# Six 1024x1024 projections as seven half-size block products, z and gates ahead of the mixers

## The chip, the cores and the metric

The kernel runs on one core of one Trainium2 chip. Its time is device microseconds (us), the median of three runs: 1177.52 us before the change (1177.08 to 1180.14). The engines of the core are TensorE (PE; PEld is its weight load), VectorE (DVE), ScalarE (ACT), GpSimd (POOL) and SyncE (SP), which issues DMAs. Each runs its own instructions in the order in which they stand, and waits at an instruction until what it reads is there.

## The reference

One layer over 512 tokens of width 1024, in fp32 (cut to what matters):

```python
h = rms_norm(x, mixer_norm)
(q, k, v, g_out, a_lr, z, xbc, dt_raw, gate_a, gate_b) = split_cols(h @ w_in, IN_SPLITS)
o_a = gla_mixer(q, k, v, g_out, a_lr, ...)          # 4 heads, chunks of 64
o_b = ssd_mixer(z, xbc, dt_raw, ...)                # 4 groups, chunks of 128
#   in it: dt = softplus(dt_raw + bias), cumulative sums of dt * a
#   y = (y_diag + y_off + X * d_skip) * silu(z); a norm per group
merged = sigmoid(gate_a) * (o_a @ w_branch_a) + sigmoid(gate_b) * (o_b @ w_branch_b)
x = x + merged @ w_out
# a conv-gated MLP, a gated per-layer embedding and a last norm follow
```

z is 2048 columns wide, each gate 1024; w_branch_a and w_out are 1024x1024, w_branch_b 2048x1024.

## The kernel before

Every matmul of a projection is done in three passes: weights and activations are split into a high and a low fp32r part (`wsplit`, L164 on ScalarE and L165 on VectorE for the weights), and high x high, high x low and low x high are summed in PSUM. `proj_a` has weights as the stationary operand and gives features by tokens, `proj_b` has tokens as the stationary operand and gives tokens by features. A projection of 1024x1024 is 192 matmuls of 512 columns. Weights come from DRAM into buffers named raw, from SyncE's queue.

`strassen` does a 1024x1024 block in seven products of half-size blocks (24 matmuls each) instead of eight: it needs sums of weight quarters (L325 on GpSimd, or an adding DMA) and sums of activations by token halves (`combine`, L293 to L302). In this kernel only the down projection of the MLP uses it.

The order: norm and transposes of x (h1); the first four x tiles of group 0 and the dt columns (psdt); on VectorE a chain of some twenty operations from psdt to the decays (L726 to L757), a transpose of its result (psq, L761), its copy qt (L762) and a small product (pscd, L764); then per group the core `ssd_core` (per chunk: yo, yd and st on TensorE; the state S is handed from chunk to chunk), `ssd_z` (the z columns of that group, `proj_b`), `ssd_branch` of the group before (ob), and `ssd_gate` (product with silu(z), a norm on GpSimd, transposes ot into ob). Then GLA with two pairs of heads (att, kst, o, u, oaT; the norms ors on GpSimd), the merge gates (`gate_pair`, whose second gate is multiplied with accb on GpSimd, L977), `branch_pair`, and w_out.

The order on each engine is made by a scheduler from the order in the code and from priorities: `ahead(n)` puts what stands in it forward by n steps, and where an instruction waits, ready work of lower priority is put before it. The buffers of a pool limit what can be put forward: four PSUM banks (mm_ps) for projections, four (sm_ps) for all else and for the block products, four weight splits.

## Time and profile before

| what | value |
|---|---|
| median of three runs | 1177.52 us |
| the profiled execution's own time | 1180.49 us |
| its span | 1178.5 us |
| TensorE busy, share | 1157.1 us, 98% |
| VectorE busy, share | 677.4 us, 57% |
| ScalarE busy, share | 520.5 us, 44% |
| GpSimd busy, share | 171.1 us, 15% |
| DMA, mean | 100 GB/s |

The profile is of one execution; its span is 2.0 us shorter than that execution's time. A busy share is an average over stages. A matmul's own duration in a group of the profile overlaps with its neighbours', so the pace of matmuls is read from how many a window holds. What an engine waited for stands in brackets in the timeline, and the chain of waits goes from the last instruction back to what released it.

### The profile page before, as it was taken

Reading aid. Unit: us, or ns where it says so; the run is one execution under the profiler, and the core shown is the slowest. Engines: PE = TensorE matmul, PEld = TensorE weight load, DVE = VectorE, ACT = ScalarE, POOL = GpSimd, SP = SyncE. Lnnn points to the kernel's source line nnn. Section 1 sums busy time; section 2 is a strip of 40 time slices with the busy share of each in tenths; the row PEclk is TensorE's granted clock in tenths of the full one; section 3 lists DMA queues with packets and bytes.
Section 4 is the critical chain, followed back from the end, with each engine's and each line's share of the span. In section 5 each row is a group of like instructions: output and inputs, shape, how many; then the busy total and the mean of one; then the engine's idle time right before and its main releaser. Section 6 shows DMA issues by size and latency. Waiting matters only on the chain.

```text
span 1178.5 us, 14049 instructions
## 1 busy us (share of the span) xinstructions
PE 1157.1 (98%) x5540; PEld 957.9 (81%) x5540; DVE 677.4 (57%) x864; ACT 520.5 (44%) x850; POOL 171.1 (15%) x175
## 2 busy tenths in 40 slices
PE   6999999999999999999999999999999999999997
PEld 6887887887887678888888888898888888888786
DVE  5767638667558537234234324565566755766764
ACT  4566373582383217442433222444434443344553
POOL 6103004022004000000011110100021000201313
PEclk9998999999999999999999999999999999999999
DMA  7332122222223134322224232752526453445221
GB/s 209 108 106 72 37 73 72 72 72 72 89 65 98 36 110 140 107 72 72 72 72 120 77 107 72 186 154 81 134 72 170 119 158 90 116 129 123 90 90 71
DMA packets 150177, 117.39 MB, mean 100 GB/s; under 512 B 5456, under 2 KB 124880, under 8 KB 150112
## 3 DMA queue, kind: packets, MB, share of 16 engines
q1 hardware_dynamic: 146624, 108.64, 31.6%
q0 software_dynamic: 2912, 5.77, 2.9%
q10 hardware_dynamic: 576, 2.10, 0.5%
q8 instruction: 43, 0.70, 0.3%
q14 instruction: 22, 0.18, 0.0%
HBM read 114.40 MB, written 2.10 MB: 99 GB/s over the span
## 4 chain that ended last, share of the span: by engine, by line
PE 96%; DVE 1%; DMA 1%; SPq 1%; POOL 1%; issue 0%; ACT 0%; POOLq 0%; ACTq 0%
PE pa L170 18%; PE pa L169 18%; PE pa L171 17%; PE pb L249 8%; PE pb L251 8%; PE pb L250 8%; PE yd L624 3%; PE sX L348 2%; PE sX L349 2%; PE sX L350 2%; PE st L632 1%; PE yo L621 1%; PE sZ L348 1%; PE sZ L349 1%; PE sZ L350 1%; DMA raw<-in_w_in_dram 1%
## 5 line engine op out<-in xcount | busy, mean ns | idle before, releaser
L165 DVE TENSOR_TENSOR wlo<-raw,whi 128x1024 fp32r<-128x1024 f32 (+1 forms) x208 | 261.5, 1263 | 255.2 <-ACT whi L164 255.0
L164 ACT CAST whi<-raw 128x1024 fp32r<-128x1024 f32 (+1 forms) x209 | 216.9, 1039 | 359.5 <-PE pa L170 219.2
L169 PE MATMUL pa<-h1h,whi 128*128 128x512 f32 (+1 forms) x416 | 160.5, 386 | 0.3 <-ACT h1h L419 0.3
L171 PE MATMUL pa<-h1h,wlo 128*128 128x512 f32 (+1 forms) x416 | 157.7, 379 | 0.0
L170 PE MATMUL pa<-h1l,whi 128*128 128x512 f32 (+1 forms) x416 | 157.0, 377 | 0.1
L169 PE MATMUL pa<-h2h,whi 128*128 128x512 f32 (+1 forms) x384 | 142.7, 372 | 0.0
L170 PE MATMUL pa<-h2l,whi 128*128 128x512 f32 (+1 forms) x384 | 142.6, 372 | 0.0
L171 PE MATMUL pa<-h2h,wlo 128*128 128x512 f32 (+1 forms) x384 | 142.3, 372 | 0.0
L249 PE MATMUL pb<-whi,h1h 128*128 128x512 f32 x256 | 99.7, 394 | 0.8 <-DVE accb L684 0.8
L250 PE MATMUL pb<-wlo,h1h 128*128 128x512 f32 x256 | 99.8, 390 | 0.0
L251 PE MATMUL pb<-whi,h1l 128*128 128x512 f32 x256 | 99.4, 392 | 0.0
L169 PEld LDWEIGHTS pa<-h1h,whi 128*128 128x128 f32 x416 | 79.9, 192 | 15.3 <-issue 1.2
L170 PEld LDWEIGHTS pa<-h1l,whi 128*128 128x128 f32 x416 | 79.6, 191 | 14.7 <-issue 1.0
L171 PEld LDWEIGHTS pa<-h1h,wlo 128*128 128x128 f32 x416 | 79.5, 191 | 13.8 <-issue 0.2
L171 PEld LDWEIGHTS pa<-h2h,wlo 128*128 128x128 f32 x384 | 72.3, 188 | 12.6
L169 PEld LDWEIGHTS pa<-h2h,whi 128*128 128x128 f32 x384 | 72.3, 188 | 12.5
L170 PEld LDWEIGHTS pa<-h2l,whi 128*128 128x128 f32 x384 | 72.3, 188 | 12.3
L249 PEld LDWEIGHTS pb<-whi,h1h 128*128 128x128 f32 x256 | 48.1, 188 | 10.6 <-DVE accb L684 1.2
L251 PEld LDWEIGHTS pb<-whi,h1l 128*128 128x128 f32 x256 | 48.1, 188 | 9.8
L250 PEld LDWEIGHTS pb<-wlo,h1h 128*128 128x128 f32 x256 | 48.1, 188 | 9.3
L549 DVE SCALAR_TENSOR_TENSOR acc<-pa,prm,acc 128x511 f32<-128x511 f32 (+2 forms) x72 | 52.6, 743 | 2.9 <-ACT acc L547 2.0
L170 PE MATMUL pa<-obl,whi 128*128 128x512 f32 x128 | 51.9, 406 | 0.0
(378 smaller groups left out, 1995.3 us busy)
## 6 DMA issues: line engine op xcount, KB each, us to landing
raw<-in_w_in_dram SPq DMA_DIRECT2D x48, 512.0 KB, 5.1
raw<-in_w_ffn_up_dram SPq DMA_DIRECT2D x44, 512.0 KB, 5.3
raw<-in_w_in_dram SPq DMA_DIRECT2D x16, 1024.0 KB, 5.1
raw<-in_w_ffn_down_dram SPq DMA_DIRECT2D x10, 1024.0 KB, 5.2
raw<-in_w_branch_b_dram SPq DMA_DIRECT2D x32, 256.0 KB, 4.1
raw<-in_w_branch_a_dram SPq DMA_DIRECT2D x8, 512.0 KB, 4.7
raw<-in_w_out_dram SPq DMA_DIRECT2D x4, 1024.0 KB, 5.1
raw<-in_w_ffn_down_dram POOLq DMA_DIRECT2D x4, 1024.0 KB, 8.6
```

The costliest lines, as they stand in the source:

```text
L164: S.copy(hi, raw)
L165: eng.tensor_tensor(lo, raw, f32(hi), op=ALU.subtract)
L169: TE.matmul(ps, lhsT=lh, rhs=rh, start=first, stop=False)
L170: TE.matmul(ps, lhsT=lh, rhs=rl, start=False, stop=False)
L171: TE.matmul(ps, lhsT=ll, rhs=rh, start=False, stop=last)
L249: TE.matmul(pss[t], lhsT=a, rhs=hi[:, kk, :], start=first, stop=False)
L250: TE.matmul(pss[t], lhsT=a, rhs=lo[:, kk, :], start=False, stop=False)
L251: TE.matmul(pss[t], lhsT=b, rhs=hi[:, kk, :], start=False, stop=last)
L348: TE.matmul(ps, lhsT=a_h, rhs=hi[:, k % 2, :], start=new and k == 0, stop=False, skip_group_check=True)
L349: TE.matmul(ps, lhsT=a_h, rhs=lo[:, k % 2, :], start=False, stop=False, skip_group_check=True)
L350: TE.matmul(ps, lhsT=a_l, rhs=hi[:, k % 2, :], start=False, stop=k == kh - 1, skip_group_check=True)
L549: V.scalar_tensor_tensor(out=acc[:, s:], in0=ps[:, : T - s], scalar=cw[:, ct, 3 - s : 4 - s], in1=acc[:, s:], op0=ALU.mult, op1=ALU.add,)
```

## The change

Six projections now go through `strassen`: z in two blocks of 1024 columns, both gates, w_branch_a and w_out. For the four of them that start from h1, `project_out` runs all 28 products right after the dt chain, applies silu or sigmoid and stores the results in DRAM (zd, gad, gbd) from ScalarE's queue; `ssd_z` now only loads them, and the gates are loaded before the merge. The sums of activations over token halves are made from h1 at the start (hpair and `combine` with parts 3 and 5), from the GLA output oa, and from the merged tiles. The order of the seven products is new (`ORDER`), and all four weight quarters are loaded once and summed in place on GpSimd (`weights_once`). Branch b is done by `proj_b`, so accb, the merge and branch a lie tokens by features; the merged tiles are transposed (mT) for w_out. The first value tiles and output gates of GLA (v0, sg0) are written where the last group's next projection would have stood. Norms of x2 are done by tile as tiles become complete. The diff, cut:

```diff
+    ORDER = (0, 4, 1, 3, 2, 5, 6)
+    def combine(pool, g2, at, j, cs=(0, 3, 2, 5)):
...
+        def tmp():
+            return pool.tile([P, 2, 256], F32, tag="cmb", name=f"cmb{uid()}", bufs=2)
+        def put(c, n, src):
+            h, l, c = at(c)
+            c = slice(c, c + 2) if n == 2 else c
+            S.copy(h[:, c, j, :], src)
+            V.tensor_tensor(l[:, c, j, :], src, f32(h[:, c, j, :]), op=ALU.subtract)
+        if 0 in cs:
+            put(0, 2, a1)
+        if 3 in cs:
+            t = tmp()
+            V.tensor_tensor(t[:, 0, :], a22, a21, op=ALU.subtract)
+            V.tensor_tensor(t[:, 1, :], t[:, 0, :], a1[:, 0, :], op=ALU.add)
+            put(3, 1, t[:, 0, :])
+            h, l, c = at(4)
+            S.activation(h[:, c, j, :], t[:, 1, :], AF.Copy, scale=-1.0)
+            V.scalar_tensor_tensor(
+                out=l[:, c, j, :], in0=t[:, 1, :], scalar=-1.0, in1=f32(h[:, c, j, :]),
+                op0=ALU.mult, op1=ALU.subtract,
+            )
+        if 2 in cs:
+            put(2, 1, a22)
+        if 5 in cs:
+            t = tmp()
+            V.tensor_tensor(t[:, 0, :], a1[:, 0, :], a21, op=ALU.subtract)
+            V.tensor_tensor(t[:, 1, :], a22, a1[:, 1, :], op=ALU.subtract)
+            V.tensor_tensor(t[:, 1, :], t[:, 1, :], t[:, 0, :], op=ALU.add)
+            put(5, 2, t)
...
+    def weights_once(r, v, n, kh):
+        if not r:
+            for q in ("11", "12", "21", "22"):
+                r[q] = new_raw(kh)
+                nc.sync.dma_start(r[q], quarter(v, q))
+        dst, src = {0: ("11", 0), 4: ("21", 0), 1: ("11", "12"), 3: ("22", 0), 2: ("11", "22"), 5: ("12", "22"), 6: ("11", "21")}[n]
+        if src:
+            pool_sum(r[dst], r[src], kh)
+        return r[dst]
...
-        for n, (c, parts, b, th, h, sign) in enumerate(STEPS):
+        for n in ORDER if once else range(7):
+            c, parts, b, th, h, sign = STEPS[n]
             with ahead():
-                raw = r[parts] if parts in r else weights(r, v, parts, kh)
+                raw = weights_once(r, v, n, kh) if once else weights(r, v, parts, kh)
...
+    def project_out(off, fn, dst):
+        cnt, pcs = Parts(), {}
+        def add(t, h, ps, sign, n):
+            first, last = cnt(t, h)
+            if first:
+                pcs[t, h] = piece_of(f"pj{uid()}")
+            pc = pcs[t, h]
+            if first and last:
+                S.activation(pc, ps, fn)
+            elif first:
+                S.activation(pc, ps, AF.Copy, scale=float(sign))
+            else:
+                V.tensor_tensor(pc, pc, ps, op=ALU.add if sign > 0 else ALU.subtract)
+                S.activation(pc, pc, fn)
+            if last:
+                nc.scalar.dma_start(dst[t][h], pc)
+        return strassen(w_in[:, off : off + 1024], hget, 4, add)
...
-        proj_b(
-            w_in[:, OFF_Z + 512 * g : OFF_Z + 512 * (g + 1)], hT, KD,
-            lambda t, ps: S.activation(sz[t], ps, AF.Silu),
-        )
+        for t in range(NT):
+            nc.sync.dma_start(sz[t], zd[g // 2][t][g % 2])
...
-        def emit(n, ps):
+        def emit(t, h, ps):
             if g == 0:
-                S.copy(accb[:, n, :], ps)
+                accb[t][h] = piece_of(f"accb{t}_{h}")
+                S.copy(accb[t][h], ps)
             else:
-                V.tensor_tensor(accb[:, n, :], accb[:, n, :], ps, op=ALU.add)
-        proj_a(
-            [w_branch_b[512 * g : 512 * (g + 1), n * P : (n + 1) * P] for n in range(KD)],
-            st[g]["ob"], 4, emit,
-        )
+                V.tensor_tensor(accb[t][h], accb[t][h], ps, op=ALU.add)
+        for h in range(2):
+            proj_b(
+                w_branch_b[512 * g : 512 * (g + 1), 512 * h : 512 * h + 512], st[g]["ob"], 4,
+                lambda t, ps: emit(t, h, ps), tail=True,
+            )
...
+    for j in range(4):
+        pr = hsp.tile([P, 2, T], F32, tag="pair", name=f"hpair{j}", bufs=1)
+        V.tensor_tensor(pr, f32(hT[0][:, 2 * j : 2 * j + 2, :]), f32(hT[1][:, 2 * j : 2 * j + 2, :]), op=ALU.add)
+        combine(hsp, pr, h_at, j, (3, 5))
+    for off, fn, dst in (
+        (OFF_Z, AF.Silu, zd[0]), (OFF_Z + 1024, AF.Silu, zd[1]), (OFF_GA, AF.Sigmoid, gad), (OFF_GB, AF.Sigmoid, gbd),
+    ):
+        for _ in project_out(off, fn, dst):
+            pass
...
+        else:
+            here = tc.cur_priority
...
-    tc.cur_priority = base + 1200
+    tc.cur_priority = base + 3000
     ssd_branch(SG - 1)
+    sx.close()
+    gvp = ggx.enter_context(tc.tile_pool(name="gvp", bufs=1, reuse_waits="tile"))
+    ring(ggx, 2)
+    tc.cur_priority = here
+    v0 = gvp.tile([P, NT, 512], F32, tag="v", name="v0", bufs=2)
+    gla_v(0, v0)
+    sg0 = [gvp.tile([P, T], F32, tag="sg", name=f"sg0_{t}", bufs=6) for t in range(NT)]
+    gla_g(0, sg0)
...
-    gates = {}
-    def gate_pair(n0):
-        def emit(i, ps):
-            n, ab = n0 + i % 2, i // 2
-            pool, tag = (mtp, "sg") if n0 % 4 else (bcp, "bc")
-            s = pool.tile([P, T], F32, tag=tag, name=f"sgt{ab}_{n}", bufs=4)
-            S.activation(s, ps, AF.Sigmoid)
-            if ab == 1:
-                G.tensor_tensor(s, s, accb[:, n, :], op=ALU.mult)
-            gates[ab, n] = s
...
+    for h in range(2):
+        for t in range(NT):
+            gb = gtp.tile([P, T], F32, tag="gt", name=f"gb{t}_{h}", bufs=6)
+            nc.sync.dma_start(gb, gbd[t][h])
+            G.tensor_tensor(accb[t][h], accb[t][h], gb, op=ALU.mult)
...
+    for j in (2, 3):
+        combine(cmbp, oa[:, 2 * j : 2 * j + 2, :], m_at, j, (0, 3))
+    for j in range(4):
+        combine(cmbp, oa[:, 2 * j : 2 * j + 2, :], m_at, j, (5, 2))
...
+    def merged(t, h):
+        ps = mm_ps(f"mT{t}_{h}")
+        for k in range(4):
+            TE.transpose(ps[:, k * P : (k + 1) * P], accb[t][h][:, k * P : (k + 1) * P], ident)
+        S.copy(mT[:, 4 * h : 4 * h + 4, t * P : (t + 1) * P], ps.rearrange("p (k t) -> p k t", k=4))
+        if t % 2:
+            for j in (2 * h, 2 * h + 1):
+                combine(cmbp, mT[:, 2 * j : 2 * j + 2, :], m_at, j, (0,) if t == 1 else (3, 5))
+            if (t, h) == (3, 0):
+                for j in range(4):
+                    combine(cmbp, mT[:, 2 * j : 2 * j + 2, :], m_at, j, (2,))
...
+    def add_a(t, h, ps, sign, n):
+        first, last = mcnt(t, h)
+        if first:
+            if t % 2 == 0:
+                tms[t // 2, h] = tmp_.tile([P, 2, T], F32, tag="tm", name=f"tm{t}_{h}", bufs=3)
+            ga = gas[t, h] = gtp.tile([P, T], F32, tag="gt", name=f"ga{t}_{h}", bufs=6)
+            nc.sync.dma_start(ga, gad[t][h])
+        tm, ga, ac = tms[t // 2, h][:, t % 2, :], gas[t, h], accb[t][h]
+        if first and last:
+            V.tensor_tensor(tm, ps, ga, op=ALU.mult)
+        elif first:
+            S.activation(tm, ps, AF.Copy, scale=float(sign))
+        else:
+            V.tensor_tensor(tm, tm, ps, op=ALU.add if sign > 0 else ALU.subtract)
+            (V if n > 2 and n != 4 else G).tensor_tensor(tm, tm, ga, op=ALU.mult)
+        if last:
+            V.tensor_tensor(ac, ac, tm, op=ALU.add)
+            merged(t, h)
+    for _ in strassen(w_branch_a, combs(m_at), 4, add_a):
+        pass
...
+    def add_o(t, h, ps, sign, n):
+        _, last = ocnt(t, h)
+        V.tensor_tensor(x2[t][h], x2[t][h], ps, op=ALU.add if sign > 0 else ALU.subtract)
+        if last:
+            onm.ready(t, h)
+    for _ in strassen(w_out, combs(m_at), 4, add_o):
+        pass
```

At the start, on TensorE, in the kernel before: psq (the transpose of the dt chain's result) stands among projections (pb is z of group 0, pa an x tile).

```order
L249 MATMUL pb19_841<-whi25_858,h1h_92 128x512
L250 MATMUL pb19_841<-wlo25_859,h1h_92 128x512
L251 MATMUL pb19_841<-whi25_858,h1l_93 128x512
L761 MATMUL psq_574<-ident_73,dt_Q_534 128x128 x4
L169 MATMUL pa28_972<-h1h_92,whi27_968 128x512
L170 MATMUL pa28_972<-h1l_93,whi27_968 128x512
L171 MATMUL pa28_972<-h1h_92,wlo27_969 128x512
```

And after: psdt is the last dt matmul, xt are transposes of two x tiles, sX26 is the first block product of z.

```order
L180 MATMUL psdt_526<-h1h_94,wlo11_523 48x512
L628 MATMUL xt_0_498<-ident_75,acc0_492 128x128 x4
L628 MATMUL xt_1_510<-ident_75,acc1_504 128x128 x4
L867 MATMUL psq_594<-ident_75,dt_Q_554 128x128 x4
L870 MATMUL pscd_600<-qt_246,ident_75 128x128
L406 MATMUL sX26_681<-whi24_673,h1h_94 128x512
L407 MATMUL sX26_681<-wlo24_674,h1h_94 128x512
L408 MATMUL sX26_681<-whi24_673,h1l_95 128x512
```

The projections between psdt and psq are gone from that place; z comes behind psq and pscd as block products.

In the core of group 3, on TensorE, before: yo, yd and st of chunk 2, and behind them matmuls of group 2's output product (obh2, obl2).

```order
L621 MATMUL yo3_2_2826<-S3_1_2815,CT3_2412 128x512
L624 MATMUL yd3_2_2828<-xdt3_2_2824,L3_2_2634 128x64 x8
L632 MATMUL st3_2_2839<-xdc3_2_2837,Btok3_2622 128x512
L170 MATMUL pa138_3074<-obl2_2588,whi137_3070 128x512
L171 MATMUL pa138_3074<-obh2_2587,wlo137_3071 128x512
L169 MATMUL pa138_3074<-obh2_2587,whi137_3070 128x512
L170 MATMUL pa138_3074<-obl2_2588,whi137_3070 128x512
```

After: the end of group 2's output product (pb237), the whole core from chunk 0 to chunk 3, and the first transpose of its gated result (ot3_0).

```order
L260 MATMUL pb237_3815<-whi240_3822,obl2_3458 128x512
L715 MATMUL yd3_0_3650<-xdt3_0_3648,L3_0_3502 128x64 x8
L723 MATMUL st3_0_3661<-xdc3_0_3659,Btok3_3492 128x512
L712 MATMUL yo3_1_3670<-S3_0_3663,CT3_3282 128x512
L715 MATMUL yd3_1_3672<-xdt3_1_3668,L3_1_3503 128x64 x8
L723 MATMUL st3_1_3683<-xdc3_1_3681,Btok3_3492 128x512
L712 MATMUL yo3_2_3696<-S3_1_3685,CT3_3282 128x512
L715 MATMUL yd3_2_3698<-xdt3_2_3694,L3_2_3504 128x64 x8
L723 MATMUL st3_2_3709<-xdc3_2_3707,Btok3_3492 128x512
L712 MATMUL yo3_3_3722<-S3_2_3711,CT3_3282 128x512
L715 MATMUL yd3_3_3724<-xdt3_3_3720,L3_3_3505 128x64 x8
L761 MATMUL ot3_0_3896<-ident_75,Xg3_3280 128x128
```

The output product of group 2 stands wholly before the core; nothing but the core's own instructions stands between yd3_0 and ot3_0.

On GpSimd, around the norms of GLA heads 2 and 3 (ors2 and ors3; the second number is the half), before: sgt1 are the products of the second merge gate with accb.

```order
L356 TENSOR_SCALAR ors2_0_4362<-oss2_0_4361 128x2
L357 TENSOR_TENSOR ors2_0_4362<-ors2_0_4362,neghalf_78 128x2
L356 TENSOR_SCALAR ors2_1_4382<-oss2_1_4381 128x2
L357 TENSOR_TENSOR ors2_1_4382<-ors2_1_4382,neghalf_78 128x2
L977 TENSOR_TENSOR sgt1_0_4593<-sgt1_0_4593,accb_235 128x512
L977 TENSOR_TENSOR sgt1_1_4625<-sgt1_1_4625,accb_235 128x512
L356 TENSOR_SCALAR ors3_0_4440<-oss3_0_4439 128x2
L357 TENSOR_TENSOR ors3_0_4440<-ors3_0_4440,neghalf_78 128x2
```

After: accb times gb, the gate loaded from DRAM, by token tile and column half.

```order
L446 TENSOR_TENSOR ors2_0_5121<-ors2_0_5121,neghalf_80 128x2
L1130 TENSOR_TENSOR accb0_0_2568<-accb0_0_2568,gb0_0_5250 128x512
L1130 TENSOR_TENSOR accb1_0_2582<-accb1_0_2582,gb1_0_5253 128x512
L1130 TENSOR_TENSOR accb2_0_2596<-accb2_0_2596,gb2_0_5256 128x512
L445 TENSOR_SCALAR ors2_1_5141<-oss2_1_5140 128x2
L1130 TENSOR_TENSOR accb3_0_2610<-accb3_0_2610,gb3_0_5259 128x512
L1130 TENSOR_TENSOR accb0_1_2638<-accb0_1_2638,gb0_1_5262 128x512
L445 TENSOR_SCALAR ors3_0_5193<-oss3_0_5192 128x2
L1130 TENSOR_TENSOR accb1_1_2652<-accb1_1_2652,gb1_1_5265 128x512
L446 TENSOR_TENSOR ors2_1_5141<-ors2_1_5141,neghalf_80 128x2
L1130 TENSOR_TENSOR accb2_1_2666<-accb2_1_2666,gb2_1_5268 128x512
L1130 TENSOR_TENSOR accb3_1_2680<-accb3_1_2680,gb3_1_5271 128x512
```

All eight products now stand between the first norm of head 2 and the last norms; before, two did.

## Rows read from the trace of the kernel before

**Rows 1.** The page: engines' busy us, and shares of the chain that ended last.
```profile
PE 1157.1 (98%) x5540; PEld 957.9 (81%) x5540; DVE 677.4 (57%) x864; ACT 520.5 (44%) x850; POOL 171.1 (15%) x175
...
PE 96%; DVE 1%; DMA 1%; SPq 1%; POOL 1%; issue 0%; ACT 0%; POOLq 0%; ACTq 0%
```

**Rows 2.** Window, steady stage: length, busy of PE, PEld, DVE, ACT, POOL.
```profile
810.00:840.00 30.00, 30.00 (x134) 24.83 (x133) 19.87 (x32) 13.06 (x21) 1.52 (x1) 1.00 0.52 140
```

**Rows 3.** Chain, around one norm's transposes: start us, us, what.
```profile
757.74 0.87 PE x2n1T L417 x8
```

**Rows 4.** Groups by form: line, engine, operation, shapes, count, busy us, mean ns.
```profile
L165 DVE TENSOR_TENSOR wlo<-raw,whi 128x1024 fp32r<-128x1024 f32 x200 | 256.6, 1287 | 249.4 <-ACT whi L164 249.2
...
L325 POOL TENSOR_TENSOR raw<-raw,raw 128x1024 f32<-128x1024 f32 x10 | 24.7, 2469 | 106.7 <-DVE wlo L165 106.7
...
L549 DVE SCALAR_TENSOR_TENSOR acc<-pa,prm,acc 128x511 f32<-128x511 f32 x24 | 17.8, 743 | 2.1 <-ACT acc L547 2.0
...
L977 POOL TENSOR_TENSOR sgt<-sgt,accb 128x512 f32<-128x512 f32 x8 | 14.1, 1768 | 76.6 <-ACT sgt L975 76.6
...
L295 DVE TENSOR_TENSOR cmb<-g 128x256 f32<-128x256 f32 x11 | 4.6, 422 | 0.2
```

**Rows 5.** The page: DMA issues, count, KB each, us to landing.
```profile
raw<-in_w_in_dram SPq DMA_DIRECT2D x16, 1024.0 KB, 5.1
```

**Rows 6.** Tiles psdt and psq: count, duration ns, first and last start us.
```profile
L171 PE MATMUL psdt<-h1h,wlo x8: 387/391/396, 41.7 to 46.6; 128*48 128x512 f32 x8
...
L761 PE MATMUL psq<-ident,dt_Q x4: 270/272/272, 80.4 to 80.7; 128*128 128x128 f32 x4
```

**Rows 7.** Four windows, columns as in Rows 2, then clock, DMA share, GB/s.
```profile
49.00:80.00 31.00, 31.00 (x143) 25.65 (x142) 25.60 (x33) 18.66 (x24) 0.00 (x0) 1.00 0.29 74
103.00:124.00 21.00, 18.74 (x73) 13.46 (x72) 19.09 (x25) 7.24 (x11) 11.91 (x9) 0.76 0.18 51
355.00:386.00 31.00, 31.00 (x153) 24.47 (x151) 24.82 (x29) 9.75 (x16) 12.17 (x8) 1.00 0.27 81
595.00:630.00 35.00, 35.00 (x168) 28.83 (x167) 11.84 (x16) 13.11 (x25) 7.24 (x7) 1.00 0.29 78
```

**Rows 8.** Timeline of VectorE at the start: start us, us, engine, line, operation.
```profile
26.79 0.68 DVE L420 TENSOR_TENSOR h1l<-xn3T,h1h 128x512 fp32r<-128x512 f32 x1
...
51.59 3.34 DVE L731 RECIPROCAL dt_s<-dt_s 32x512 f32<-32x512 f32 x1
...
75.81 0.68 DVE L757 TENSOR_TENSOR dt_q<-dt_s,dt_x 32x512 f32<-32x512 f32 x1 [1.92 <-ACT dt_s L756]
...
81.04 0.69 DVE L762 COPY qt<-psq 128x512 f32<-128x512 f32 x1 [0.70 <-PE psq L761]
```

**Rows 9.** Timeline of all engines beside two GpSimd sums of the MLP's weights.
```profile
1003.04 1.83 DVE L296 TENSOR_TENSOR cmb<-cmb,g 128x256 f32<-128x256 f32 x1
...
1006.24 2.39 POOL L325 TENSOR_TENSOR raw<-raw,raw 128x1024 f32<-128x1024 f32 x1 [1.65 <-DVE wlo L165]
...
1006.68 3.04 DVE L165 TENSOR_TENSOR wlo<-raw,whi 128x1024 fp32r<-128x1024 f32 x1
```

**Rows 10.** Timeline of TensorE, first state of group 0.
```profile
113.85 2.08 PE L621 MATMUL yo<-S,CT 128*128 128x512 f32 x2 [0.68 <-ACT S L635]
```

**Rows 11.** Chain through the end of the core of group 3.
```profile
358.67 1.73 PE yd L624 x16
...
387.86 0.70 DVE Xg L647
...
393.12 1.62 PE ot L670 x13
...
395.51 1.20 PE pa L169 x4
```

**Rows 12.** Timeline of GpSimd, a norm of head 3.
```profile
619.13 0.69 POOL L356 TENSOR_SCALAR ors<-oss 128x2 f32<-128x2 f32 x1 [5.57 <-ACT on L936]
619.91 0.70 POOL L357 TENSOR_TENSOR ors<-ors,neghalf 128x2 f32<-128x2 f32 x1
```

More of the change, by code (lines that the diff above doesn't have):

```diff
@@ L353, in strassen, with __init__, __call__, ready @@
             yield
+    class Parts:
+        def __init__(self):
+            self.left = {}
+        def __call__(self, t, h):
+            total = 1 if (t // 2, h) == (1, 0) else 2
+            n = self.left.get((t, h), total)
+            self.left[t, h] = n - 1
+            return n == total, n == 1
+    class TileNorms:
+        def __init__(self, pool, tag, bufs, x, gain, dst, name):
+            self.a = pool, tag, bufs, x, gain, dst, name
+            self.nm = {}
+        def ready(self, t, h):
+            pool, tag, bufs, x, gain, dst, name = self.a
+            first = t not in self.nm
+            if first:
+                self.nm[t] = Norm(pool, x[t], f"{name}{t}", tag, bufs)
+            self.nm[t].square(h)
+            if first:
+                self.nm[t].gather()
+            else:
+                norm_T(self.nm[t], gain, dst, t)
     def rsqrt_mean(dst, ssq, inv, n):
```

315 lines of the change are left out of this document (147 added, 168 removed).

## The prediction

> **What bounds the kernel now.** I read the page's busy shares and its chain first: TensorE is busy 98% of the span, and 96% of the chain that ended last is TensorE's own work [rows 1]. Then the stretches by windows: in a steady stage 134 matmuls of 512 columns fill 30 us with nothing idle, so one costs 30 / 134 = 0.224 us [rows 2]; the 0.39 us that the groups show as a mean is the length of one pipelined record and is not used. So removed matmuls are time removed, and anything that leaves TensorE without an instruction it may run is time added. VectorE (57%), ScalarE (44%) and GpSimd (15%) bound nothing on average [rows 1]; they count only where TensorE's in-order queue stands behind one of their results. In the kernel before such places are filled with other projections: TensorE is busy for all of 49 to 80 us while VectorE works out dt, all of 355 to 386 us in the last SSD core, and all of 595 to 630 us around the last two GLA heads [rows 7]. The change takes its matmuls from just these fillers, so I read the new TensorE order at these places.
>
> **What TensorE saves.** Six 1024x1024 blocks (z twice, two gates, branch a, output) go from 192 matmuls to 7 x 24 = 168: 6 x 24 = 144 fewer, 144 x 0.224 = 32.3 us. Added are 32 transposes of the merged tiles; eight cost 0.87 us [rows 3], so 32 cost 3.5. Net -28.8 us. Branch b keeps its count.
>
> **What the other engines gain in work.** 36 more weight splits at 1.29: 46 us of VectorE, and a cast on ScalarE for each. 48 more weight sums on GpSimd at 2.47: 119 us [rows 4]. Token combinations, pairs and adds, some 45 us of VectorE. All engines stay far below the span, so none of this is on the path by its amount. The 32 stores and 32 loads of 256 KB are 17 MB; at the 5.1 us in which 1 MB lands [rows 5] that is 87 us of one queue, hidden under 1,100 us of matmuls, so I cost them at nothing.
>
> **Start-up.** Before, the dt matmuls end at 47.0 us and psq, the transpose that waits for the dt chain, runs at 80.4; 33 us of x and z projections lie between [rows 6, 7]. After, TensorE's row has only two x transposes between psdt and psq, and the first block product comes behind psq and pscd. So when is psq ready? VectorE is free of h1l at 26.79 + 0.68 = 27.5 us [rows 8]. In its order before dt's last result now stand: four pair sums of 1024 columns (4 x 1.29 = 5.2), 28 operations of 256 columns at 0.42 (11.8) and four of 512 at 0.69 (2.8), 12 convolution steps at 0.74 (8.9), five splits (5.5) and dt's own 22 operations, 16.4 us with the 3.34 of the reciprocal (the other 21 take 0.41 to 1.21) [rows 4, 8]. That is 50.6 us, so 78.1 at best; with 4.4 us from the last product to psq as before (75.81 to 80.2 [rows 6, 8]) and qt's 0.69 and pscd the first block product starts about 83. From 47.0 TensorE has 1.3 us of small work there: 34 us idle. Two things add: GpSimd's first sums run beside the chain. A VectorE operation of 256 columns with two SBUF inputs that takes 0.42 took 1.83 beside a sum, and a split took 3.04 instead of 1.23, ending only after the sum [rows 4, 9]; four sums could cost 4 x 1.6 = 6. And the splits and casts interleave, which could win a few us back. I take 34. Bounds: 21, if the dt chain alone counts (47 + 16.4 + 6 of ScalarE's steps and psq), and 46.
>
> **Block products of z and gates.** Per block GpSimd has 8 x 2.4 = 19 us and VectorE 14 x 1.23 = 17, against 168 x 0.224 = 37.6 of TensorE; weights are loaded through five buffers at 5.1 us each [rows 5]. Hidden; I take 2 us for block boundaries (0 to 24, rival three).
>
> **Core of group 0.** The last two chunks, then its gate, stand in TensorE's row without filler; before, only the first two did. One hand-off from a state's copy to the next yo is 0.7 us of idle [rows 10], 1.2 with an addition on VectorE (0.69) for the copy, and the gate chain costs 5.3 us (below). I take 6 (0 to 9).
>
> **Core of group 3.** Before, it took from yd3_0 at 358.7 to the first product of ob3 at 395.5, with 96 matmuls of ob2 in it (21.5 us). After, ob2 is used up before yd3_0, and v and the output gates of GLA come later than ob3. Bare chain: three state hand-offs at 1.2 (3.6), then from yd3_3's end 387.85 over Xg, the norm on GpSimd and Xg to the transposes at 393.12 (5.3), and from ot's end (393.12 + 1.62) to the first product (0.8) [rows 11]. 9.7 idle; I take 9 (4 to 15).
>
> **GLA heads 2 and 3.** Before, the merge gates filled them. After, att2 to the last oaT stand together: 60 small matmuls and transposes, 13 us if they keep 0.22 each. On GpSimd the order between the norms of head 2 and 3 holds eight gate multiplications: 8 x 1.77 = 14.1 us [rows 4], while a norm itself takes 0.69 + 0.70 [rows 12] and had a free engine before. So the last norm ends about 10 + 14.1 + 4 x 1.2 = 29 us after att2, and on, oaT, its copy and the combination of the last tokens follow (4 us): branch a's first product starts at 33 instead of 13. SyncE's queue says the same: branch a's weights are issued behind the loads of gb and ga, which wait for the multiplications (24 + 5.1 landing + split 2.3). I take 20 (4, if the multiplications fall into gaps, to 28).
>
> **Merge and output.** Between branch a's last product and w_out's, copies (0.62), casts and sums of 0.42 hang on the last transposes; fillers of 12 products stand between them. I take 5 (0 to 12).
>
> **Clock.** In 103 to 124 us, around TensorE's waits for the first state, the granted clock was 0.76 [rows 7, 10]: part of the stretch was at 1.2 GHz instead of 2.4. 21 x 0.24 = 5 us of lost clock there, part of it while idle. After the three long waits I take 2 each, 6 (0 to 15). The Trainium skill, "TensorE: Matmul & The Clock Gate", "What's actually happening", says that the clock halves once the array has been idle and comes back after sustained work; by it all three waits are followed by a slow stretch, against none by the rows of 595 to 630, where TensorE never idled. The row of 103 to 124 sides with it.
>
> **Sum.** 1178.5 - 28.8 + 34 + 2 + 6 + 9 + 20 + 5 + 6 = 1231.7 us of span, 1233.7 with the 2.0 around it. The profiled execution (1180.49) was 3.0 over the median of 1177.52, so I predict 1230.7, said as 1230: slower by 4.5%.
>
> **Rivals.**
> First, half covered (1199): the start-up stays (31), but GpSimd's multiplications slip into gaps while head 2 is in its matmuls, so heads cost 8, core 3 five, all else 6: 1178.5 - 28.8 + 50 - 1.0. For it: GpSimd stood idle 5.6 us before a norm of head 3 [rows 12], room for three multiplications. Against: GpSimd's order is fixed, with the later norms behind them.
> Second, not slower (1177): the waits are at their floor. The place is start-up: if dt's chain on VectorE and ScalarE runs bare, the token sums slotting into its gaps, psq comes at about 69 and TensorE idles 21; with 7 elsewhere the losses are 28 and eat the saving exactly: 1178.5 - 28.8 + 28 - 1.0. Each us by which psq is earlier is one us; faster than before begins below 69. For it: VectorE had 5.4 us idle in 49 to 80 [rows 7]. Against: 31 us of VectorE's new and old work stand ahead of dt's first operation in its order.
> Third, preparation becomes the bound (1255): GpSimd and VectorE don't overlap where both read two SBUF inputs [rows 9], so a product with a sum costs 4.9 + 2.5 = 7.4 us of the two against 5.4 of TensorE; 24 such products, 2.0 us each, are 48 us if nothing is prepared ahead, and half of that, 24, if one product is. For it: the rows beside a sum. Against: of seven products three need no sum, and a whole block fits (36 against 37.6). The Trainium skill, "GPSIMD Engine Reference", "1. Specifications", states that GpSimd's way to SBUF is shared with VectorE and contended by VectorE's instructions with two SBUF inputs; by it this rival is the likelier one, by the block's sum mine is.
>
> **Chances.** Forecast 0.63 (own range 1207 to 1252), half covered 0.15, not slower 0.14, preparation bound 0.08. A measurement of this kernel can tell 0.3% (3.5 us) from no change: below 1174 faster, above 1181 slower. The second rival spreads 10 us to both sides: faster 0.06, same 0.05, slower 0.03 of it; a saving through a cause I don't see gets another 0.02 of faster from the forecast's share. Faster 0.08, same 0.05, slower 0.87. The range of 8 in 10 leaves out most of the second rival and the top of the third: 1185 to 1260.
>
> **What would show it.** Right: TensorE's windows empty from about 50 to 83 us, no z matmul before psq; holes of some us between yd3_0 and the first ob3 product; a hole of 15 to 20 us before branch a's first product, with GpSimd's multiplications between two norms; TensorE's busy time near 1,128. Wrong: psq before 69; TensorE full in the last core; a hole in the block products that ends on a split. If TensorE's idle total is under 29 us beyond before's, the sign is wrong.

## The result, and the profile after

The changed kernel takes 1293.09 us (1291.15 to 1295.55, four runs), the kernel before beside it 1178.82. The ratio is 1.097, with a 95% interval of 1.094 to 1.100: slower by 114 us. Slower was forecast, at 1230 us; the time lies 33 us over the upper end of the range. The profiled execution has a span of 1293.4 us.

The page after has the line that answers to the first of [rows 1] (busy us, share and count by engine); the chain that ended last is now 75% PE and 14% DVE.

```profile
PE 1166.8 (90%) x5428; PEld 953.3 (74%) x5428; DVE 849.2 (66%) x1043; ACT 591.5 (46%) x957; POOL 303.0 (23%) x227
```

TensorE has 112 instructions fewer and is still busy 9.7 us longer, and it idles 126.6 us instead of 21.4. What it idled on stands in the view of its waits (engine, line, releaser: us in total, times, longest):

```profile
PE psq L867 <- ACT dt_Q L864: 17.9, 1, 17.9
PE xt L628 <- ACT acc L625: 15.3, 2, 10.8
PE ot L761 <- DVE Xg L755: 12.9, 2, 7.5
PE sZ L406 <- ACT cah L311: 11.4, 2, 11.2
PE sZ L406 <- DVE pj L654: 9.2, 7, 2.7
PE sY L407 <- DVE wlo L174: 7.5, 1, 7.5
...
PE oaT L1107 <- DVE on L1100: 6.3, 3, 3.1
```

No single wait is the loss: every place at which z and the gates used to fill TensorE's queue now has one, and block products (sZ, sY) wait as well. The windows by stage, columns as in [rows 7]: start-up, most of the block products of z and the gates, the core of group 3, the merge with the output projection.

```profile
49.00:83.00 34.00, 2.23 (x8) 1.43 (x8) 31.44 (x46) 13.02 (x21) 1.74 (x1) 0.55 0.00 0
86.00:256.00 170.00, 160.77 (x684) 130.01 (x684) 114.19 (x80) 90.38 (x113) 80.23 (x36) 0.97 0.40 132
...
510.00:544.00 34.00, 23.78 (x98) 17.26 (x97) 19.88 (x30) 6.08 (x13) 11.55 (x11) 0.65 0.10 31
...
751.00:865.00 114.00, 86.42 (x342) 67.37 (x343) 105.99 (x114) 49.15 (x73) 54.60 (x26) 0.85 0.39 119
```

In the first, VectorE fills 31.4 of 34 us and TensorE 2.2, where it ran 143 matmuls before [rows 7]. In the last, VectorE is the full engine (106 of 114), and the clock is 0.85.

To compare stages I took the time from one landmark of TensorE to the next, and subtracted its own work, counted from its instructions at full pace (0.224 us a matmul of 512 columns [rows 2], 0.109 a transpose [rows 3], yd, yo and st as in undisturbed chunks). The rest is idle time and slow pace together:

| stage, up to | rest before | rest after | more | predicted |
|---|---|---|---|---|
| first block product (psq before) | 15.9 | 53.2 | 37.3 | 34 (+2 clock) |
| first product of the core of group 0 | 2.7 | 20.4 | 17.7 | 2 |
| its transposes ot0 | 6.1 | 12.9 | 6.8 | 6 (+2 clock) |
| ot3, cores 1 to 3 | 4.8 | 25.4 | 20.6 | 9 (+2 clock) |
| att2 (GLA heads 0 and 1) | 7.8 | 11.0 | 3.2 | 0 |
| branch a's first product (heads 2 and 3) | 3.0 | 16.5 | 13.5 | 20 |
| first transposes of x2n | 1.5 | 41.2 | 39.7 | 5 |
| the end | 14.6 | 19.7 | 5.1 | 0 |

They add to 143.9; less the 28.8 us that TensorE saves this is 115.1, against 114.9 by the spans. Predicted were 82.

Part of each rest is TensorE at half clock. Cut into windows of 2 us, busy time times one minus the granted clock comes to 34.4 us after, in 13 stretches, and 4.8 us in one stretch before. One of them, TensorE's timeline (start, us, operation, [idle before, releaser]):

```profile
140.94 0.39 PE L408 MATMUL sZ<-whi,hcl 128*128 128x512 f32 x1
143.98 0.50 PE L406 MATMUL sZ<-whi,hch 128*128 128x512 f32 x1 [2.65 <-DVE pj L654]
144.32 0.57 PE L407 MATMUL sZ<-wlo,hch 128*128 128x512 f32 x1
...
146.39 0.63 PE L406 MATMUL sZ<-whi,hch 128*128 128x512 f32 x1
146.82 0.63 PE L407 MATMUL sZ<-wlo,hch 128*128 128x512 f32 x1
...
148.21 0.40 PE L408 MATMUL sZ<-whi,hcl 128*128 128x512 f32 x1
148.44 0.40 PE L406 MATMUL sZ<-whi,hch 128*128 128x512 f32 x1
```

Starts lie 0.43 us apart until 147.7 and 0.23 afterwards, 1.2 and then 2.4 GHz: a wait of 2.65 us has cost 1.7 us more. VectorE's timeline of the same place shows why the bank was late:

```profile
139.89 3.44 DVE L174 TENSOR_TENSOR wlo<-raw,whi 128x1024 fp32r<-128x1024 f32 x1 [1.64 <-ACT whi L173]
143.25 0.68 DVE L654 TENSOR_TENSOR pj<-pj,sY 128x512 f32<-128x512 f32 x1
```

The split took 3.44 instead of 1.22 us beside a GpSimd sum; the eviction pj, which frees the bank for sZ, stood behind it.

The core of group 3 [rows 11] has the same pattern:

```profile
510.86 1.90 PE L715 MATMUL yd<-xdt,L 128*128 128x64 f32 x16
...
521.16 2.08 PE L712 MATMUL yo<-S,CT 128*128 128x512 f32 x2 [3.04 <-DVE S L732]
523.02 3.52 PE L715 MATMUL yd<-xdt,L 128*128 128x64 f32 x16
...
540.11 2.15 PE L761 MATMUL ot<-ident,Xg 128*128 128x128 f32 x9 [5.49 <-DVE Xg L755]
```

yd takes 3.52 us for the same 16 records as 1.90 before: from 520 to 544 us 8.0 us went to half clock beside 7.7 of idle time.

In the merge, GpSimd and VectorE beside each other, with the first product of branch a that waits for them:

```profile
752.64 5.55 POOL L354 TENSOR_TENSOR raw<-raw,raw 128x1024 f32<-128x1024 f32 x1 [8.45 <-DVE wlo L174]
752.76 0.42 DVE L332 TENSOR_TENSOR cmb<-oa 128x256 f32<-128x256 f32 x1
...
755.51 0.41 DVE L332 TENSOR_TENSOR cmb<-oa 128x256 f32<-128x256 f32 x1
755.96 2.52 DVE L333 TENSOR_TENSOR cmb<-cmb 128x256 f32<-128x256 f32 x1
758.15 2.57 POOL L354 TENSOR_TENSOR raw<-raw,raw 128x1024 f32<-128x1024 f32 x1
758.40 2.87 DVE L312 TENSOR_TENSOR cbl<-cmb,cbh 128x512 fp32r<-128x512 f32 x1
760.68 2.79 POOL L354 TENSOR_TENSOR raw<-raw,raw 128x1024 f32<-128x1024 f32 x1
761.30 2.45 DVE L331 TENSOR_TENSOR cmb<-oa 128x256 f32<-128x256 f32 x1
763.43 2.51 POOL L354 TENSOR_TENSOR raw<-raw,raw 128x1024 f32<-128x1024 f32 x1
763.67 3.35 DVE L174 TENSOR_TENSOR wlo<-raw,whi 128x1024 fp32r<-128x1024 f32 x1
...
767.09 0.80 PE L407 MATMUL sY<-wlo,cah 128*128 128x512 f32 x1 [7.49 <-DVE wlo L174]
```

The four VectorE operations from 755.96 on take 2.5 to 3.4 us each, where the same forms take 0.41 to 1.22 alone. Each of them ends 0.3 to 1.1 us behind the end of a sum, about its own length. The holding up goes both ways: from 752.76 to 755.92 six operations ran at their full pace while the first sum was open, and that sum took 5.55 us where the next three took 2.5 to 2.8 (GpSimd's spans are rough in the profile).

The longest wait of this stage comes later, behind the last transposes of branch a's result:

```profile
841.26 0.80 PE L406 MATMUL sZ<-whi,cah 128*128 128x512 f32 x1 [11.20 <-ACT cah L311]
```

There the first sZ product of w_out waits for the token combinations of the last merged tiles, which VectorE works off behind splits and additions.

### The profile page after: what moved, and what is told of

It is laid out like the page before. It is cut to its first block, busy times and chain, and to the rows that moved or that the text cites. A ratio compares the mean times of both kernels' runs of the same rounds, so it can differ in the third digit from the quotient of the medians.

```text
span 1293.4 us, 14283 instructions
## 1 busy us (share of the span) xinstructions
PE 1166.8 (90%) x5428; PEld 953.3 (74%) x5428; DVE 849.2 (66%) x1043; ACT 591.5 (46%) x957; POOL 303.0 (23%) x227
## 4 chain that ended last, share of the span: by engine, by line
PE 75%; DVE 14%; issue 4%; ACT 4%; POOL 1%; DMA 1%; SPq 1%; POOLq 0%; DVEq 0%; ACTq 0%
PE pa L179 10%; PE pa L178 10%; PE pa L180 10%; PE pb L258 6%; PE pb L260 6%; PE pb L259 6%; DVE wlo L174 5%; PE sX L406 4%; PE sX L407 4%; PE sX L408 4%; PE sZ L406 2%; PE sZ L407 2%; PE sZ L408 2%; PE yd L715 1%; ACT whi L173 1%
## 5 line engine op out<-in xcount | busy, mean ns | idle before, releaser
L174 DVE TENSOR_TENSOR wlo<-raw,whi 128x1024 fp32r<-128x1024 f32 (+1 forms) x244 | 351.7, 1448 | 212.4 <-ACT whi L173 207.3
L173 ACT CAST whi<-raw 128x1024 fp32r<-128x1024 f32 (+1 forms) x245 | 253.6, 1038 | 278.5 <-PE pa L179 130.6
L354 POOL TENSOR_TENSOR raw<-raw,raw 128x1024 f32<-128x1024 f32 (+1 forms) x60 | 157.9, 2642 | 291.3 <-DVE wlo L174 291.1
L178 PE MATMUL pa<-h1h,whi 128*128 128x512 f32 (+1 forms) x288 | 108.7, 377 | 1.8 <-DVE acc L616 1.7
L179 PE MATMUL pa<-h1l,whi 128*128 128x512 f32 (+1 forms) x288 | 109.5, 380 | 0.1
L180 PE MATMUL pa<-h1h,wlo 128*128 128x512 f32 (+1 forms) x288 | 107.5, 374 | 0.0
L180 PEld LDWEIGHTS pa<-h2h,wlo 128*128 128x128 f32 x384 | 73.2, 191 | 12.4
L179 PEld LDWEIGHTS pa<-h1l,whi 128*128 128x128 f32 x288 | 55.6, 193 | 10.8 <-issue 1.7
L258 PE MATMUL pb<-whi,obh 128*128 128x512 f32 x128 | 52.1, 407 | 1.2 <-ACT obh L763 0.9
L259 PE MATMUL pb<-wlo,obh 128*128 128x512 f32 x128 | 51.2, 403 | 0.0
L258 PE MATMUL pb<-whi,h1h 128*128 128x512 f32 x128 | 50.3, 397 | 0.8 <-DVE accb L776 0.8
L260 PE MATMUL pb<-whi,obl 128*128 128x512 f32 x128 | 50.9, 407 | 0.0
```

The costliest lines, as they stand in the source:

```text
L173: S.copy(hi, raw)
L174: eng.tensor_tensor(lo, raw, f32(hi), op=ALU.subtract)
L178: TE.matmul(ps, lhsT=lh, rhs=rh, start=first, stop=False)
L179: TE.matmul(ps, lhsT=lh, rhs=rl, start=False, stop=False)
L180: TE.matmul(ps, lhsT=ll, rhs=rh, start=False, stop=last)
L258: TE.matmul(pss[t], lhsT=a, rhs=hi[:, kk, :], start=first, stop=False)
```

## The experiments

Each of the first eight changes one part of the changed kernel (7 is 3 with one addition). Stages and rests are those of the table above. Experiments 2 to 8 were timed once each, and four runs of the changed kernel spread over 4.4 us, so their small differences are read from the stages and not from the total.

**1. The merge's weight sums on VectorE.**

```diff
-            G.tensor_tensor(dst[:, q, :], dst[:, q, :], src[:, q, :], op=ALU.add)
+            summer[0].tensor_tensor(dst[:, q, :], dst[:, q, :], src[:, q, :], op=ALU.add)
...
+    summer[0] = V
     for _ in strassen(w_branch_a, combs(m_at), 4, add_a):
...
+    summer[0] = G
```

> The sums of weight quarters for branch a and w_out (16 of 128x1024) move from GpSimd to VectorE; all else as in the changed kernel, whose stretch from branch a's first product to the norm of x2 took 114.6 us for 73.4 us of matmuls. Theory P (GpSimd's sums and VectorE's operations with two SBUF inputs exclude each other, so the stretch is their sum: 79.5 us of VectorE alone and 38 of GpSimd's sums): the sums cost 1.22 us each on VectorE instead of 2.4 of both, the stretch falls to 95 to 102 us, the kernel to about 1277. Rival Q (the stretch is bound by the chain of combinations behind the last transposes, on VectorE): 19.5 us more on the engine of the chain, the stretch is no shorter, the kernel 1293 to 1305.

1278.35 us; the stretch from branch a's first product to x2n takes 100.5 us instead of 114.6. The window:

```profile
751.00:851.00 100.00, 81.54 (x343) 64.23 (x344) 93.63 (x130) 49.01 (x73) 16.11 (x10) 0.89 0.43 137
```

VectorE does 16 operations more and is busy 12 us less. So GpSimd's help costs more than it gives here. The long wait before sZ stays (11.6 us).

**2. The same sums left out** (their products then use unsummed weights).

```diff
     def pool_sum(dst, src, kh):
+        if not summing[0]:
+            return
```

> The same 16 sums are left out altogether (each product of branch a and w_out uses an unsummed quarter, so the values differ). Theory P: without the sums VectorE's own 80 us bound the stretch, 78 to 88 us, the kernel about 1262. Rival Q: the chain behind the transposes stays, the stretch falls by under 8 us, the kernel stays above 1285.

1267.19 us, the stretch 90.3 us: 10 less than with the sums on VectorE, 24 less than with them on GpSimd. Its rest is still 16.9, a little over what was expected; 4.0 of it is the wait for branch a's first weights, and 7.8 the wait before sZ for the combinations of the last merged tiles. So part of rival Q's chain is there too, beside theory P.

**3. The first z block's seven products ahead of the dt chain.**

```diff
+    for off, fn, dst in (
+        (OFF_Z, AF.Silu, zd[0]),
+    ):
+        for _ in project_out(off, fn, dst):
+            pass
+
+    if True:
         go = ahead(60000)
...
-        (OFF_Z, AF.Silu, zd[0]), (OFF_Z + 1024, AF.Silu, zd[1]), (OFF_GA, AF.Sigmoid, gad), (OFF_GB, AF.Sigmoid, gbd),
+        (OFF_Z + 1024, AF.Silu, zd[1]), (OFF_GA, AF.Sigmoid, gad), (OFF_GB, AF.Sigmoid, gbd),
```

> The token sums of h1 and the first block of z stand ahead of the dt chain in the code, so that TensorE's order has 168 block matmuls between the x transposes and psq. Theory O (the start-up's 35 us of idle are TensorE's order, nothing to run before psq): the first block product starts at about 66 us, behind the second x transpose, instead of 86, and the dt chain hides behind 37 us of products: 18 to 22 us gained, about 1272. Rival V (VectorE's 58 us of work between 27 and 86 bound the start either way, the products need its splits and token sums): products stall on splits, under 6 us gained, above 1287.

1288.79 us. The block products start at 65.6 instead of 86.1 us, but psq then waits 14.7 us at 124.3: a mask that the dt chain needs is made on GpSimd, and it now stood behind the weight sums. The time is the one that rival V gives, but not by its cause: the edit put a new wait in place of the old one. It decides nothing between the two theories, and experiment 7 takes this wait out. (`go = ahead(60000)` opens the dt chain.)

**4. Seven of the eight gate products with accb on GpSimd left out** (those tiles stay without their gate).

```diff
-            G.tensor_tensor(accb[t][h], accb[t][h], gb, op=ALU.mult)
+            if (t, h) == (0, 0):
+                G.tensor_tensor(accb[t][h], accb[t][h], gb, op=ALU.mult)
```

> Seven of the eight products of accb and gb on GpSimd are left out (the loads stay; values differ). Theory G (the 16.5 us lost between att2 and branch a's first product come from GpSimd's order, the norms of heads 2 and 3 behind eight products of 1.25): the last norm ends 7 to 9 us earlier and branch a's first product starts about 8 us earlier, 1285. Rival W (that product waits for its weights, whose loads are late for another reason): last norm earlier, first product within 2 us of before, about 1292.

1285.86 us, theory G's number, but only half of it came where G put it. Branch a starts at 746.9 instead of 750.9 us: the products are 4 us of this stage's 13.5, and another 4 fall away in the merge. TensorE's wait for branch a's first weights grew from 4.0 to 5.8 us, which is rival W's part. What remains of the stage's rest is 12.6 against 3.0 before; experiment 8 has more on it.

**5. The pair of banks of Z among the projections' banks.**

```diff
-                banks[b] = [sm_ps(f"s{b}{uid()}") for _ in range(2)]
+                bank = mm_ps if once and b == "Z" else sm_ps
+                banks[b] = [bank(f"s{b}{uid()}") for _ in range(2)]
```

> The third pair of partial sums of a block product (Z) takes PSUM banks of the projections instead of the four that X and Y fill. Theory B (of the 18 us lost from the first block product to the first core, most are TensorE's waits for the additions that free a bank, 9.2 us of idle before Z products, and the stretches at half clock that follow them): the waits vanish, 12 to 17 us gained, about 1279. Rival E (the losses there come from GpSimd's sums and VectorE's splits excluding each other): the waits move to the splits, under 5 us gained, above 1288.

1280.80 us. The rest of the block products of z and gates falls from 20.4 to 6.2, and TensorE is full where 9.2 us were idle:

```profile
86.00:256.00 170.00, 170.00 (x746) 140.13 (x747) 114.67 (x87) 97.17 (x121) 83.82 (x36) 0.99 0.45 149
```

The seven waits of sZ were for a free bank, and with one more pair late evictions do no harm. The merge gets 5 us worse (46.3). Z shares those banks with mT there; experiment 10, which leaves the merge's Z where it was, doesn't show this loss.

**6. z projected in its cores, as before.**

```diff
-        for t in range(NT):
-            nc.sync.dma_start(sz[t], zd[g // 2][t][g % 2])
+        proj_b(
+            w_in[:, OFF_Z + 512 * g : OFF_Z + 512 * (g + 1)], hT, KD,
+            lambda t, ps: S.activation(sz[t], ps, AF.Silu),
+        )
```

> z as before the change: 96 matmuls per group within that group's stage, nothing stored in DRAM; gates, branch a and w_out stay block products. 48 matmuls more (+10.8 us). Theory F (the losses of the cores of groups 0 and 3, 7 and 20 us, and a good part of the 18 us in the block products are z's absence as filler and its blocks): from the first ot to that of group 3 no loss, core 3 back to about 5 us, two blocks' waits less: -20 -5 -9 + 10.8 = -23, about 1270. Rival K (the cores lose by slower VectorE and GpSimd, whatever fills TensorE): core 3 keeps over 12 us of its 20, the kernel above 1290.

1260.51 us, although TensorE has 48 matmuls (10.8 us) more. The rest is 0.8 in the core of group 0 (12.9 with the change), 5.7 in cores 1 to 3 (25.4), and 9.0 in the block products that are left. So z's absence cost 31.8 us in the cores and its blocks another 11.4, against the 10.8 that its product form saves.

**7. Experiment 3 with the mask made ahead of the sums.**

```diff
         psdt = ps
+        smask = piece_of("smask", 32)
+        G.memset(smask, 1.0)
+        G.memset(smask.rearrange("p (c l) -> p c l", c=NT)[:, :, 0:1], 0.0)
...
     hc = [hsp.tile([P, 4, 4, 256], R, name=f"hc{c}") for c in "hl"]
```

> As the run with a z block ahead of the dt chain, where psq still waited 14.7 us because a GpSimd memset of the scan's mask stood behind weight sums; the mask is now written ahead of the block. Theory O (order alone makes the start-up's loss): no wait at psq, the first block product still at 66 us, 14.7 us plus its slow restart gained on that run, 18 to 21 on the changed kernel, about 1273. Rival V (VectorE's work is the bound at the start): the wait turns up at the splits or token sums of the first block, above 1284.

1272.36 us, as expected. psq waits no more. What is left of the start-up are the two waits of xt, 15.3 us, for ScalarE's part of the first x tiles.

**8. Branch a and the output projection as plain products** (token layout kept).

```diff
-    for _ in strassen(w_branch_a, combs(m_at), 4, add_a):
-        pass
+    for h in range(2):
+        proj_b(w_branch_a[:, 512 * h : 512 * h + 512], ca, KD, lambda t, ps: add_a(t, h, ps), tail=h == 1)
...
-    for _ in strassen(w_out, combs(m_at), 4, add_o):
-        pass
+    for h in range(2):
+        proj_b(w_out[:, 512 * h : 512 * h + 512], cb_, KD, lambda t, ps: add_o(t, h, ps), tail=h == 1)
```

> Branch a and w_out as plain projections by tokens (192 matmuls each; no weight sums, no token sums; merged tiles still transposed), gates and z still block products. 48 matmuls more, +10.8 us. Theory P (the merge's 41 us of loss are the block products' preparation on VectorE and GpSimd): the stretch from branch a's first product to the norm of x2 takes 84 to 90 us instead of 114.6, for 84 of matmuls; about 1266. Rival Q (it loses on the accb, transpose, copy hand-offs of the token layout, which stay): the stretch stays above 105, the kernel above 1283.

1276.70 us, between the two expectations. The stretch takes 102.3 us for 83.7 of work:

```profile
744.00:846.00 102.00, 91.49 (x390) 73.56 (x391) 45.79 (x51) 23.23 (x33) 17.10 (x15) 0.94 0.37 131
```

VectorE is busy 46 of 102 us, so preparation bounds nothing any more, and 18.6 us are still lost where the kernel before loses 1.5. This part of the loss isn't the block products'; experiment 12 looks for it. Branch a also starts 7.0 us earlier here (743.8): without the token combinations of its input, TensorE's waits before oaT fall from 6.3 to 1.8 us. So the combinations held up heads 2 and 3 as well as the gate products did, as far as this run tells them from the weights and buffers that change with them.

**9. Experiments 5 to 8 together** (bank pair for the gates only, the first gate's product ahead of the dt chain instead of z's).

```diff
+                bank = zbank if zbank and b == "Z" else sm_ps
...
+    for _ in project_out(OFF_GA, AF.Sigmoid, gad):
+        pass
...
-        (OFF_Z, AF.Silu, zd[0]), (OFF_Z + 1024, AF.Silu, zd[1]), (OFF_GA, AF.Sigmoid, gad), (OFF_GB, AF.Sigmoid, gbd),
+    for _ in project_out(OFF_GB, AF.Sigmoid, gbd):
```

> Four parts undone at once: z is projected in its cores as before, branch a and the output projection are plain, the remaining block products (the two gates) have their Z pair in the projection's banks, and the first gate's product stands ahead of the dt chain with the mask made early. Of the saving on TensorE only two products are left (2 x 24 x 0.224 = 10.8 us). If the losses stand in separate places and add up, the time is the changed kernel's 1293 less what each mend gave alone: 32.6 (z in place), 20.7 (product ahead of dt), 16.4 (plain branch a and output) and some 5 of the bank pairs, since half of the block products are left: 1218 (1208 to 1228). If nearly all that the change lost came from these parts, the losses beyond TensorE's work fall to what the kernel before had, about 57: 1111 + 57 = 1168 and 2 around it, 1170. If the mends share their gains (two of them pay for the same wait), it is above 1232.

1225.69 us, 1.041 of the time before (1.036 to 1.045): the losses stand in separate places and very nearly add (1218 expected, up to 1228). But the changed kernel's losses aren't all in these parts: 1170 is far off. 33 us of rest are left at the start and 19 in the merge.

**10. All seven products kept, three mends** (experiments 1, 5 for z and gates, 7).

```diff
+            summer[0].tensor_tensor(dst[:, q, :], dst[:, q, :], src[:, q, :], op=ALU.add)
...
+        return strassen(w_in[:, off : off + 1024], hget, 4, add, zbank=mm_ps)
```

> All seven block products stay. Mended are: the Z pair of the z and gate products in the projection's banks, the first z product ahead of the dt chain with the mask made early, and branch a's and the output's weight sums on VectorE. Adding up what each gave alone (12.3, 20.7 and 14.7 from 1293) gives 1245; with VectorE, which then has more to do in the merge stretch while the Z pair shares banks with the merged tiles' transposes (that cost 5 us alone), up to 1255. If the three gains overlap, above 1260. Under 1181, and so no slower than the kernel before, it comes only if the stages of core 3 and of the heads lose nothing either, for which nothing speaks.

1249.44 us, in the expected span: the three gains add as well. The merge takes 101.2 us, against 100.5 in experiment 1.

**11. More work for TensorE in the core of group 3.**

```diff
+                if g == SG - 1 and c == NT - 1:
+                    again = mm_ps("again")
+                    for j in range(3 * HPG):
+                        j %= HPG
+                        TE.matmul(
+                            again[:, j * 64 : (j + 1) * 64], lhsT=L[:, j, :], rhs=xdt[:, j * 64 : (j + 1) * 64],
+                            start=True, stop=True,
+                        )
...
+                    if g == SG - 1:
+                        again = mm_ps("again")
+                        for _ in range(3):
+                            TE.matmul(again, lhsT=Bt[:, c, :], rhs=xdc, start=True, stop=True)
```

> The changed kernel with more work on TensorE in the core of group 3: 9 matmuls of 512 columns and 24 of 64 columns whose results nobody reads stand between its chunks, and by that the scheduler puts most of group 2's output product (95 matmuls) behind yd3_3, ahead of the transposes ot3_0. All sums and results of the layer stay. If the stage loses its time because TensorE's queue has nothing to run while the states and the gate are worked out (theory F: no filler, and the half clock that follows each hole), then the 5.5 us wait before ot3_0, the waits of 3.0 and 0.9 before yo and most of the 8 us at half clock between 520 and 544 us go, and the kernel gets faster although it does some 4 us more: 1293 - 12 = 1281 (1277 to 1286), with TensorE full through the last core. If the gate's chain is held by VectorE (rival V: ob2's additions now fall into the gate's chain and make it later), the wait only moves behind ob2 and the time is 1291 to 1299.

1303.84 us: slower, and neither theory's number. The added matmuls cost four times what I had reckoned, 8.0 + 2.7 + 2.1 + 3.5 = 16.3 us by their rows: their operands are plain fp32, and each one runs as two records. Some 2.6 us of the 8.0 are half clock. The stage grew by 12.0, so without them it is 2 to 4 us shorter. From 512 us on TensorE is full at clock 1.00, the wait ahead of ot3 is gone, and there is no half clock in the core:

```profile
505.00:510.00 5.00, 5.00 (x23) 3.05 (x22) 0.00 (x0) 0.00 (x0) 1.70 (x2) 0.92 0.00 0
510.00:515.00 5.00, 4.27 (x24) 2.87 (x24) 3.46 (x5) 1.31 (x3) 3.68 (x3) 1.00 0.00 0
...
535.00:540.00 5.00, 5.00 (x23) 4.02 (x22) 2.81 (x6) 0.35 (x1) 0.00 (x0) 1.00 0.02 3
```

That part is as theory F had it, and ob2's additions held nothing up. But ob2's product had filled another hole, the preparation of the core. Now nine waits of 0.2 to 3.5 us stand there, 8.6 in all, with 4.7 us at half clock, one of them behind GpSimd:

```profile
500.59 8.00 PE L735 MATMUL again<-xdc,Btok 128*128 128x512 f32 x12 [3.47 <-POOL xdc L729]
```

The filler that was left can fill one of the two holes; with z in its place both are filled (experiment 6).

**12. Experiment 9 with each merged tile's transposes one tile later.**

```diff
-        merged(t, h)
+        if late:
+            merged(*late.pop())
+        late.append((t, h))
```

> The kernel with four parts undone (1225.7 us), and the transposes of each merged tile written behind the next tile's branch product instead of behind its own. It tells what the layout by tokens costs when no block product is in the merge: that kernel waits 8.9 us before five of its transposes (0.6 + 1.7 + 1.7 + 1.6 + 3.5) for the gate product and the addition on VectorE, and runs 1.7 us slower at half clock after two of them. If these waits are the loss of that stage, all but the last one go: 1225.7 - 5.5 - 2 = 1218 (1216 to 1221). If the transposes are only waited for by something else that is late anyway (the split of the last merged tile ahead of the output projection), 1224 to 1227.

1220.17 us, within what was expected; the transposes' waits fall from 8.9 to 4.1 us and the stage's rest from 18.9 to 12.4. So a third of the loss in a merge without block products was the hand-off of each tile from TensorE over VectorE to its own transposes, which the layout by tokens brought in. What the other 12.4 are wasn't tried out; 3.3 of it are the wait for the first weights and 4.1 the last transposes. It is the fastest of these kernels and 1.037 of the time before (1.031 to 1.042): no version here beats the kernel before.

## Why the prediction was right in sign and wrong in size

**TensorE's saving** was right as a count: 112 instructions fewer, 28.8 us at full pace. The busy time foreseen, near 1,128 us, was 1166.8. Of the 38.5 us between them 29.6 are matmuls at half clock, which count as busy for twice as long; the other 9 weren't followed.

**Start-up** was right within 3 us: the first block product started at 86.1, for about 83, and the stage lost 37.3, for 34 and 2 of clock. In the hole TensorE first waits for x tiles (15.3) and then for psq (17.9); experiment 7, which puts products ahead of the dt chain, gets 20.7 of it back.

**Core 0** was right (6.8). **Heads 2 and 3** were over-sized, 13.5 for 20, and the number lies in the range (4 to 28) more by luck than by its mechanism. The gate products took 1.27 us each where the sum had 1.77 [rows 4], and without seven of them only 4 us went; 7.0 go in experiment 8, which makes no token combinations of branch a's input.

**The step that failed is "Merge and output", "I take 5 (0 to 12)": it was 39.7.** I sized it as a few hand-offs between transposes. Two things stood there instead. The larger is the sums: VectorE was busy for 106 of 114 us, held up beside GpSimd's sums. Experiment 1 takes 14.1 us out by moving them onto VectorE itself, experiment 2 24.3 by leaving them out. This is the mechanism of my third rival. The second is the chain behind the last merged tiles, which the step named and priced too low: one wait of 11.2 us before sZ, still 7.8 with the sums left out. Experiment 8 shows 22.6 us gone with the block products. Of the 18.6 then left, experiment 12 gives 6.5 to the hand-off of the merged tiles, which the token layout brought in; for the other 12 only two waits are known (3.3 and 4.1), and the cause stays open.

I had weighed the third rival with a block's sum, 36 against 37.6 us, that holds for z and the gates (experiment 5) but not here: the merge has the token combinations, the gate products and the additions on VectorE as well. A stage has to be summed with all of the engine's work in it. I had this work in the list under "What the other engines gain", 46 and 45 us of VectorE, at no cost, and VectorE was busy 171.8 us longer. The Trainium skill, "GPSIMD Engine Reference", "1. Specifications", counts VectorE's instructions with two SBUF inputs among those contended with GpSimd; the rows of 755.96 to 763.67 agree with it.

**Block products**, 2 taken, 17.7 measured. It was within the bounds given (0 to 24), but not by preparation running out: experiment 5 fills TensorE with the same sums and splits, by one more pair of banks. A delayed split delays the eviction behind it, and the next product finds no bank.

**Core 3**, 9 (and 2 of clock) taken, 20.6 measured, 15 the upper bound. The hand-offs were counted rightly in sum: 0.7, 3.0 and 0.9 for three of 1.2, and 5.5 for 5.3. Another 8.0 are half clock while the core runs. Experiment 6 removes all but 1 of the 20.6 with the filler.

**Clock**, "after the three long waits I take 2 each, 6 (0 to 15)": 29.6 us more than before. The price of one stretch was right (1.4 to 3.7 in twelve of the 13, 8.0 in the core of group 3); their number wasn't, since waits of 2.7 us, and chains of short waits as at 510 to 540, can be followed by one as well. The waits and the clock are one loss: a hole costs its length and, where such a stretch follows, about 2 us.

In sum: 82 forecast, 143.9 measured; of the 62 between them 35 are the merge, 16 the block products and 10 core 3 with its clock.

## What to carry to other kernels

A projection with nothing waiting for it is worth its time as a filler: before it is made cheaper or moved, list the holes that it fills, each with its length and some 2 us of half clock that may follow (z saved 10.8 us as products and cost 43.4, so 32.6 on balance). When work is put on GpSimd, sum VectorE's work in that very stage, and count an operation on two SBUF operands that starts beside a GpSimd sum at what is left of the sum and its own length. Here the block products of z and the gates lacked PSUM banks, not engine time (experiment 5), and those of the merge lacked VectorE's time (experiments 1 and 2).

## What the runs showed of the hardware

A VectorE operation of 128x256 on two SBUF operands took 2.5 us when it started beside a GpSimd sum, against 0.41 alone: it ended about its own length behind the sum. The Trainium skill, "SBUF — State Buffer", "Who interferes with whom", says that such an instruction contends with a GpSimd instruction that reads SBUF, and that the order of issue decides which of the two is blocked. The rows agree: the VectorE operations at 758.40, 761.30 and 763.67 started 0.2 to 0.6 us behind a sum and waited for it, and the sum at 752.64 took 5.55 us while VectorE's operations ran at full pace. An addition with one operand in PSUM wasn't held up (0.68 us at 826.97, beside a sum from 826.79 to 829.31). With 16 sums fewer on GpSimd and 16 operations more on VectorE, VectorE was busy 12 us less (experiment 1).

After a wait of 2.65 us matmuls ran at the half clock of 1.2 GHz until 147.7 (143.98); after two others of the same length, at 187.25 and 230.47, the clock fell only after some full-speed matmuls at the first and not at all at the second. The runs don't settle what decides it.
